# Eight convolution products in place of five rotary ones at the head of a mixer

## The chip, the cores and the metric

The kernel runs on one core of a Trainium2 chip. The metric is the device time of one execution in microseconds, as the median of the runs shown. All times below are microseconds (us) unless marked ns.

## The reference, cut to what matters

Two transformer blocks are computed on 512 tokens of width 1024, in float32. The change lies in the first block's mixer, which follows its first feed-forward part:

```
u = rms_norm(h, mix_pre_g)                  # one factor per token, a gain per channel
proj = u @ w_in                             # 1024 x 4808
q_a, k_a, v_a, q_i, k_i, w_i, gate_b, gate_c, conv_in, g_a, g_b = split(proj)
q_a, k_a, q_i, k_i = (apply_rope(t) for t in ...)
y_a = dsa_attention(q_a, k_a, v_a, q_i, k_i, w_i) @ w_a_out
y_b = (gate_b * short_conv_causal(gate_c * conv_in)) @ w_b_out
merged = sigmoid(g_a) * y_a + sigmoid(g_b) * y_b
h = h + rms_norm(merged @ w_out, mix_post_g)
```

`dsa_attention` scores every earlier token with the index heads (`q_i`, `k_i`, weighted by `w_i`), keeps the 128 best per query, and attends to these alone.

## The kernel before, in words

Activations lie with channels on the 128 partitions and the 512 tokens along the row. A product of 1024 input channels with 128 output channels is eight blocks of 128 channels. Every float32 factor is split into a high and a low part, and each block is three matmuls (`mm3`, line 287), so one product over all tokens is 24 matmuls of 512 columns (`lin`, line 296), and over one half of the tokens 24 matmuls of 256 columns. Each weight tile is loaded by a DMA on the sync queue, copied to the high part on ScalarE (line 252 or 282) and split on VectorE (line 253 or 283).

A stage begins in `begin` (line 303). The residual `h` is not complete then: the stage before it left behind a post-norm of its result `f` (`due`), and the second-half products of its last five output tiles (`self.rest`). `enter` (line 604) gives for each half of the tokens a list of steps: the sum of squares of `f`, its factor, the factor turned into a row, the update of `h` and the split of `h` into the next products' inputs (`body`, lines 624 to 633), and then the same three steps for the norm of `h`. The gain goes into the split, but the factor per token, `r`, does not: the products are begun on the unscaled `h`, and whoever takes a product out of PSUM multiplies by `r`. `begin` therefore runs a few products (their number is the length of `K["lead:mix"]`, whose letters say from which pool their weights are taken) over the first half, while the norm of the second half is prepared, and then over the second half. What takes a product out of PSUM (`put`) is held back until `r` of its half exists (lines 336 to 343). PSUM has five banks for these products ("lg" 3, "mm" 2, line 141).

In the mixer (line 939) the five lead products are the keys (T_KK, attention and index keys together) and four tiles of index queries (T_QI). Each is turned by `rotated` (line 774): four ScalarE copies with swapped halves (line 785), a VectorE product with the cosine table (787), a GpSimd product with the sine table (790), a VectorE sum (791). The factor `r` is multiplied into the two tables by GpSimd (`more`, line 946), once for each half. After the lead comes T_VW (values and index weights), over all tokens, and is scaled by `r` on VectorE (line 930). Then `keys` and `heads` split the turned tiles (lines 802 to 815), the index scores are made (lines 978 to 982; line 981 needs the index weights), and four tiles of attention queries (T_QA) follow. For each of three query blocks a chain of 16 rounds on VectorE finds the 128 best scores (lines 992, 993, ended by line 994). Under it TensorE does the convolution's twelve products (lines 1002 to 1015: gate_c, conv_in and gate_b for four tiles) and the first four gate products. `gate_c * conv_in` is taken without `r`, and the square of `r` (`rr`, line 1001) is multiplied in afterwards (line 1006); the two taps are line 1012.

Then eight attention units follow, two for each of four query blocks (line 1027): logits (lines 823, 824), softmax, transposes, products with the values. The first block needs no chosen scores, block 1 needs those of the first chain, and so on. With each unit one gate product is written (`gates`, line 1046: a product, a ScalarE copy, a GpSimd product with `r` at line 928, a tanh), and the second set of eight gates comes behind the units.

The order in the text isn't the order on the engines. When the kernel is built, the framework's scheduler takes for each engine the earliest written instruction that its own model of time holds to be ready and that finds a free tile. Tiles come from pools with fixed numbers of slots: 32 of "b", 8 of "t", 5 of "u" (line 60), 5 pairs of "w4" for weights. Gates, keys, queries, scores and outputs of the attention are all "b".

Of the kernel before, what the change touches and what calls it, by code (L numbers as in the profile page):

```python
# [15 lines left out]
OP = mybir.AluOpType  # L16
# [34 lines left out]
T_KK, T_QI, T_VW, T_QA, T_CONV, T_GB, T_GA = 0, 1, 5, 6, 10, 22, 30  # L51
# [35 lines left out]
 'urg:mixsh': 1,  # L87
 'sq:mixsh': 'PV',
 'bf:mix': [0, 1, 4, 6],
 'lead:mix': 'ubbbb',  # L90
 'ahead:mix': 5,
 'late:mix': [5, 0],
 'urg:crosssf': 1,
# [85 lines left out]
class Net:  # L179
# [123 lines left out]
    def begin(self, jobs, step, fill=()):  # L303


        first, second = step(A), step(B)
        wts = []
        for (w, n, xs, k0, _), tag in zip(jobs, K["lead:" + self.phase]):
            wts.append(self.lead_weights(w, n, len(xs), k0, tag) if tag != "w" else self.weights(w, n, len(xs), k0)[0])
        todo = first["post"] + first["body"] + first["norm"][:1]  # L310
        for go in self.rest:
            if todo:
                todo.pop(0)()
            go()
        self.rest = []
        for do in todo:
            do()
        todo = (second["post"][:2] + first["norm"][1:2] + second["post"][2:] + first["norm"][2:]
                + second["body"] + second["norm"])

        def advance():
            if todo:
                todo.pop(0)()

        for go in fill:
            go()
            advance()
        for _ in range(3):
            advance()

        for tok, d in zip(HALVES, (first, second)):
            waiting = []
            for (_, _, xs, _, put), wt in zip(jobs, wts):
                waiting.append((put, self.lin(wt, xs, tok)))
                advance()
                if not any(do in todo for do in d["norm"]):
                    while waiting:
                        put, ps = waiting.pop(0)
                        put(ps, tok)
            while any(do in todo for do in d["norm"]):  # L340
                advance()
            for put, ps in waiting:
                put(ps, tok)
        for do in todo:
            do()
# [573 lines left out]
    def projection(self, w, n, xs, r, alloc=None, light=False):  # L919

        nc = self.nc
        t = (alloc or self.tmp)((P, S), F32)

        def put(ps, tok):
            if light:
                nc.scalar.copy(t[:, tok], ps)  # L926
                if r is not None:
                    nc.gpsimd.tensor_tensor(t[:, tok], t[:, tok], r[:, tok], op=OP.mult)  # L928
            else:
                nc.vector.tensor_tensor(t[:, tok], ps, r[:, tok], op=OP.mult)  # L930

        return t, (w, n, xs, 0, put)

    def project(self, *args, **kw):
# [4 lines left out]
    def mix(self):  # L939
        self.phase = "mix"  # L940
        nc, h = self.nc, self.h
        cos, sin, cm = self.table("cos1"), self.table("sin1"), self.table("causal")

        def more(tok, r, rs):
            for t in (cos, sin):
                nc.gpsimd.tensor_tensor(t[:, tok], t[:, tok], r[:, tok], op=OP.mult)

        xs, r, step = self.enter("mix_pre_g", more)
        w = "w_in"
        turns = [self.rotated(w, n, xs, cos, sin) for n in (T_KK, T_QI, T_QI + 1, T_QI + 2, T_QI + 3)]  # L950
        vw, last = self.projection(w, T_VW, xs, r)
        self.begin([j for _, j in turns], step)
        self.stream([last])
        self.attending = True
        kk = turns[0][0]
        ka, ki = self.keys(kk, 0), self.keys(kk, 1)
        qi = []
        for x, _ in turns[1:]:
            qi += self.heads(x)
        v = []  # L960
        wi = self.small("wi", [P, NT, H], 1)
        for j in range(NT):
            ps = self.pa()
            nc.tensor.transpose(ps[:, :72], vw[:72, j * P : j * P + P], self.ident[:72, :72])
            v.append(self.values(ps[:, 0:64], j))
            nc.vector.tensor_scalar(wi[:, j, :], ps[:, 64:72], float(np.float32(H ** -0.5)), None, op0=OP.mult)


        first = self.cp.tile([P, P], F32, tag="first", name="first")
        nc.gpsimd.tensor_copy(first, cm[:, 384:512])  # L970
        bias = [first]
        score = []
        for i in range(1, NT):
            n = (i + 1) * P
            sc = self.big((P, n), F32)
            for hd in range(H):
                ps = self.bank("lg")
                self.logits(ps, qi[hd], hd % 2, i, ki, n)
                t = self.tmp((P, n))
                nc.scalar.activation(t, ps[:, :n], AF.Relu, scale=0.125)  # L980
                nc.vector.scalar_tensor_tensor(
                    sc, t, wi[:, i, hd : hd + 1], cm[:, 384 - i * P :] if hd == 0 else sc, op0=OP.mult, op1=OP.add)
            score.append(sc)
        qa = []
        for t in range(4):
            x, job = self.rotated(w, T_QA + t, xs, cos, sin)
            self.stream([job])
            qa += self.heads(x)
        for sc in score:
            for _ in range(TOPK // 8):  # L990
                m8 = self.small("m8", [P, 8], 4)
                nc.vector.max(out=m8, in_=sc)
                nc.vector.match_replace(out=sc, in_to_replace=m8, in_values=sc, imm_value=TAKEN)
            nc.vector.tensor_scalar(sc, sc, TAKEN_BELOW, NEG, op0=OP.is_gt, op1=OP.mult)
            bias.append(sc)


        self.second = nc.gpsimd if K["conv"] == "P" else nc.vector
        bz = []
        rr = self.rowtile()  # L1000
        nc.gpsimd.tensor_tensor(rr, r, r, op=OP.mult)
        for j in range(4):
            c = self.project(w, T_CONV + 3 * j, xs, None, light=True)
            ci = self.project(w, T_CONV + 3 * j + 1, xs, None, light=True)
            nc.gpsimd.tensor_tensor(c, c, ci, op=OP.mult)
            nc.gpsimd.tensor_tensor(c, c, rr, op=OP.mult)
            tap = [self.gains[:, G_CONV + 3 * j + d : G_CONV + 3 * j + d + 1] for d in range(3)]
            z = self.tmp()
            nc.scalar.activation(z, c, AF.Copy, scale=tap[2])
            for d in (1, 0):  # L1010
                s = 2 - d
                nc.vector.scalar_tensor_tensor(z[:, s:], c[:, : S - s], tap[d], z[:, s:], op0=OP.mult, op1=OP.add)
            b = self.project(w, T_CONV + 3 * j + 2, xs, r, light=True)
            nc.gpsimd.tensor_tensor(b, b, z, op=OP.mult)
            bz.append(self.split(b, self.pair()))

        self.second = nc.vector


        ot = [self.big(dt=F32) for _ in range(4)]  # L1020
        gb, more_b = self.gates(w, T_GB, xs, r, KD)
        ga, more_a = self.gates(w, T_GA, xs, r, KD)

        for _ in range(K["gb0"]):
            next(more_b)

        def units():
            for i in range(NT):
                for g in range(2):
                    yield self.group(i, g, qa, ka, v, ot, (i + 1) * P,  # L1030
                                     lambda l, hd, j: self.softmax(l, 0.125, (i + 1) * P, bias[i], pool=K["F6"][j])), [lambda: next(more_b, None)]

        self.overlapped(units())
        for _ in more_b:
            pass
        for _ in more_a:
            pass
        self.attending = False
        self.branch(gb, "w_b_out", bz)
        merged = self.merge(gb, ga, "w_a_out", [self.split(t, self.pair(alloc=self.xt)) for t in ot])  # L1040
        f = [self.big(dt=F32) for _ in range(KD)]
        self.memory_parts()
        self.down("w_out", f, 0, merged, False, K["late:mix"])
        self.leave(f, "mix_post_g")
# [589 lines left out]
```

## Time and profile before

| | |
|---|---|
| runs | 2095.65, 2098.32, 2098.66 us, median 2098.32 |
| profiled execution | 2091.38 us, of which the span from first to last instruction is 2089.6 |
| busy, share of the span | TensorE 96%, its weight loads 85%, VectorE 74%, ScalarE 53%, GpSimd 12% |
| mean granted TensorE clock | 0.990 of full speed |
| mixer, head: lead products and T_VW | 361 to 415 us |
| mixer, scores and choice of the best | 417 to 539 us |
| mixer, attention units and gates | 539 to 640 us |

A busy TensorE in this table is one whose matmuls overlap in the profile's records; their ends are modelled. The granted clock has two levels, full and half; a value in between is a mean over a stretch.

### The profile page before, as it was taken

The numbers are of one execution on the slowest core, as the hardware profiler recorded it, in microseconds if no ns is written. First come the engines' busy times: TensorE is split into PE (matmuls) and PEld (weight loads), VectorE is DVE, ScalarE is ACT, GpSimd is POOL, SyncE is SP. The second block draws the span as 40 slices with busy tenths as digits, with TensorE's granted clock in tenths as the row PEclk, the third lists the DMA queues.
The fourth block names the chain that finished last, engine by engine and source line by source line (L and its number), as shares of the span: only waits on it lengthen the run. The fifth ranks groups of instructions, "written<-read, shape, count | busy, mean of one in ns | idle before, by whom it ended". The sixth has DMA issues, their size and how long they took to land. (4 is left out here: it accounts for less than half of the span.)

```text
span 2089.6 us, 32337 instructions
## 1 busy us (share of the span) xinstructions
PE 2011.4 (96%) x12428; PEld 1766.1 (85%) x12428; DVE 1544.4 (74%) x2956; ACT 1101.7 (53%) x2052; POOL 254.4 (12%) x239
## 2 busy tenths in 40 slices
PE   8999999899999999999999998998999999999997
PEld 7899998778778888998999998776778888988997
DVE  7977786799775585587777869588987678666755
ACT  5644454673573454554445445467864436444752
POOL 2000002313331310040000003213100000000001
PEclk9999999899999999999999999999999999999999
DMA  5233333212222233221333342211112313323331
GB/s 163 91 112 97 106 107 122 71 61 91 91 71 95 77 120 103 93 70 51 113 110 102 106 141 72 66 41 51 41 41 81 114 31 122 99 89 104 112 101 41
DMA packets 66010, 186.43 MB, mean 89 GB/s; under 512 B 6976, under 2 KB 14144, under 8 KB 65856
## 3 DMA queue, kind: packets, MB, share of 16 engines
q1 hardware_dynamic: 63376, 180.97, 26.8%
q10 hardware_dynamic: 2448, 3.41, 0.5%
q8 instruction: 97, 1.59, 0.3%
q14 instruction: 57, 0.47, 0.1%
q0 software_dynamic: 32, 0.00, 0.0%
HBM read 182.25 MB, written 2.10 MB: 88 GB/s over the span
## 5 line engine op out<-in xcount | busy, mean ns | idle before, releaser
L290 PE MATMUL mm<-x,w 128*128 128x512 f32 (+1 forms) x2064 | 473.8, 379 | 0.0
L290 PE MATMUL mm<-b,w 128*128 128x256 f32 (+1 forms) x2625 | 448.6, 322 | 2.0 <-ACT b L510 1.8
L290 PEld LDWEIGHTS mm<-x,w 128*128 128x128 f32 x2064 | 364.0, 188 | 74.9 <-DVE v L1274 0.7
L290 PEld LDWEIGHTS mm<-b,w 128*128 128x128 f32 x2625 | 375.2, 188 | 48.9 <-ACT b L510 4.2
L252 ACT CAST w<-r 128x1024 fp32r<-128x1024 f32 (+2 forms) x256 | 229.8, 898 | 277.8 <-PE mm L290 118.0
L290 PE MATMUL lg<-x,w 128*128 128x256 f32 (+1 forms) x2460 | 348.6, 295 | 6.8 <-DVE t L1385 4.7
L253 DVE TENSOR_TENSOR w<-r,w 128x1024 fp32r<-128x1024 f32 (+2 forms) x254 | 267.8, 1055 | 116.3 <-ACT w L252 111.3
L290 PE MATMUL lg<-b,w 128*128 128x256 f32 (+1 forms) x1929 | 352.9, 334 | 0.0
L290 PEld LDWEIGHTS lg<-x,w 128*128 128x128 f32 x2460 | 315.9, 188 | 27.9 <-DVE t L1385 6.4
L290 PEld LDWEIGHTS lg<-b,w 128*128 128x128 f32 x1929 | 294.5, 188 | 42.1
L457 ACT CAST w<-r 128x1024 fp32r<-128x1024 f32 x147 | 154.6, 1053 | 138.1 <-PE lg L290 81.3
L458 DVE TENSOR_TENSOR w<-r,w 128x1024 fp32r<-128x1024 f32 x147 | 178.7, 1221 | 19.9 <-ACT w L457 19.4
L290 PE MATMUL mm<-x,u 128*128 128x256 f32 x756 | 108.1, 287 | 15.6 <-ACT x L513 7.1
L510 ACT CAST b<-t 128x512 fp32r<-128x512 f32 (+1 forms) x113 | 60.8, 539 | 112.5 <-DVE t L745 34.3
L290 PEld LDWEIGHTS mm<-x,u 128*128 128x128 f32 x756 | 96.9, 193 | 18.7 <-ACT x L513 7.5
L569 POOL TENSOR_TENSOR sh<-sh,sh 128x256 f32<-128x256 f32 x45 | 37.5, 834 | 502.8 <-ACT sh L563 499.9
L511 DVE TENSOR_TENSOR b<-t,b 128x512 fp32r<-128x512 f32 (+1 forms) x113 | 67.2, 596 | 26.3 <-ACT b L510 26.0
L569 POOL TENSOR_TENSOR sf<-sf,sf 128x256 f32<-128x256 f32 x28 | 23.3, 833 | 450.4 <-ACT sf L563 440.4
L563 ACT ACTIVATE sh<-h 128x256 f32<-128x256 f32 x128 | 49.9, 411 | 52.5 <-DVE h L630 22.7
L928 POOL TENSOR_TENSOR b<-b,rows 128x512 f32<-128x512 f32 x32 | 52.5, 1642 | 174.7 <-ACT b L926 174.7
L861 DVE TENSOR_TENSOR u<-tt,u 128x512 fp32r<-128x512 f32 x92 | 62.0, 684 | 9.9 <-ACT u L860 9.3
L290 PE MATMUL lg<-x,b 128*128 128x256 f32 x456 | 68.1, 291 | 0.0
(271 smaller groups left out, 2738.9 us busy)
## 6 DMA issues: line engine op xcount, KB each, us to landing
r<-in_ffn_w SPq DMA_DIRECT2D x86, 512.0 KB, 3.3
r<-in_w_in SPq DMA_DIRECT2D x64, 512.0 KB, 3.2
r<-in_ffn_w SPq DMA_DIRECT2D x68, 256.0 KB, 2.7
r<-in_w_up SPq DMA_DIRECT2D x32, 512.0 KB, 3.2
r<-in_w_down SPq DMA_DIRECT2D x32, 384.0 KB, 3.4
r<-in_ffn_w SPq DMA_DIRECT2D x16, 384.0 KB, 3.3
r<-in_w_out SPq DMA_DIRECT2D x8, 512.0 KB, 3.2
r<-in_xattn_w_k SPq DMA_DIRECT2D x8, 512.0 KB, 3.2
```

Of the source, the lines that this page charges most:

```text
L252: nc.scalar.copy(hi, raw)
L253: self.second.tensor_tensor(lo, raw, hi.bitcast(F32), op=OP.subtract)
L290: self.nc.tensor.matmul(ps, lhsT=lhsT, rhs=rhs, start=start, stop=stop, skip_group_check=on)
L457: nc.scalar.copy(hi, raw)
L458: nc.vector.tensor_tensor(lo, raw, hi.bitcast(F32), op=OP.subtract)
L510: nc.scalar.copy(hi, src)
L511: nc.vector.tensor_tensor(lo, src, hi.bitcast(F32), op=OP.subtract)
L563: nc.scalar.activation(t, x, AF.Square)
L569: eng.tensor_tensor(ts[0], ts[0], t, op=OP.add)
L861: nc.vector.tensor_tensor(lo, ps[:, :n], hi.bitcast(F32), op=OP.subtract)
L928: nc.gpsimd.tensor_tensor(t[:, tok], t[:, tok], r[:, tok], op=OP.mult)
```

## The change

Eight convolution products (gate_c and conv_in of four tiles) become the lead. They need no `r`, so `begin` takes them out of PSUM at once (the mark `free`), with a ScalarE copy into a "b" tile. The tables are loaded behind the lead and multiplied by `r` over all tokens; the products `gate_c * conv_in` are taken on GpSimd at the same place. The five rotary products then follow over all tokens, and T_VW after them as before. In the convolution's loop only gate_b is left to be multiplied out.

```
- 'lead:mix': 'ubbbb',
+ 'lead:mix': 'uttbbbww',
@@ begin
-                waiting.append((put, self.lin(wt, xs, tok)))
+                ps = self.lin(wt, xs, tok)
+                if getattr(put, "free", False):
+                    put(ps, tok)
+                else:
+                    waiting.append((put, ps))
                 advance()
@@ projection
+        put.free = light and r is None
         return t, (w, n, xs, 0, put)
@@ mix
+        xs, r, step = self.enter("mix_pre_g")
+        w = "w_in"
+        conv = [self.projection(w, T_CONV + 3 * j + d, xs, None, lambda shape, dt: self.big(shape, dt), True)
+                for j in range(4) for d in range(2)]
+        self.begin([j for _, j in conv], step)
+        conv = [t for t, _ in conv]
         cos, sin, cm = self.table("cos1"), self.table("sin1"), self.table("causal")
-        def more(tok, r, rs):
-            for t in (cos, sin):
-                nc.gpsimd.tensor_tensor(t[:, tok], t[:, tok], r[:, tok], op=OP.mult)
-        xs, r, step = self.enter("mix_pre_g", more)
-        w = "w_in"
+        for t in (cos, sin):
+            nc.gpsimd.tensor_tensor(t, t, r, op=OP.mult)
+        for j in range(4):
+            nc.gpsimd.tensor_tensor(conv[2 * j], conv[2 * j], conv[2 * j + 1], op=OP.mult)
         turns = [self.rotated(w, n, xs, cos, sin) for n in (T_KK, T_QI, T_QI + 1, T_QI + 2, T_QI + 3)]
         vw, last = self.projection(w, T_VW, xs, r)
-        self.begin([j for _, j in turns], step)
+        self.stream([j for _, j in turns])
         self.stream([last])
...
         for j in range(4):
-            c = self.project(w, T_CONV + 3 * j, xs, None, light=True)
-            ci = self.project(w, T_CONV + 3 * j + 1, xs, None, light=True)
-            nc.gpsimd.tensor_tensor(c, c, ci, op=OP.mult)
+            c = conv[2 * j]
             nc.gpsimd.tensor_tensor(c, c, rr, op=OP.mult)
```

## Rows read from the trace of the kernel before

**Rows 1.** The page, busy time of each engine over the whole span.
```profile
PE 2011.4 (96%) x12428; PEld 1766.1 (85%) x12428; DVE 1544.4 (74%) x2956; ACT 1101.7 (53%) x2052; POOL 254.4 (12%) x239
```

**Rows 2.** Windows, head: length, busy (instructions) PE, PEld, DVE, ACT, POOL, clock, DMA.
```profile
361.14:370.71 9.57, 7.36 (x38) 6.56 (x37) 9.57 (x21) 7.10 (x17) 0.73 (x1) 0.71 0.35 110
370.71:383.72 13.01, 13.01 (x105) 12.80 (x104) 7.36 (x28) 6.13 (x14) 3.06 (x4) 0.95 0.32 111
383.72:388.15 4.43, 0.00 (x0) 0.03 (x1) 3.13 (x6) 1.94 (x5) 3.67 (x5) 0.72 0.08 33
388.15:400.86 12.71, 11.47 (x66) 10.51 (x66) 11.77 (x27) 9.76 (x23) 4.05 (x5) 0.69 0.01 1
400.86:414.79 13.93, 13.91 (x91) 12.17 (x89) 9.38 (x23) 10.86 (x27) 7.02 (x9) 1.00 0.21 75
414.79:421.65 6.86, 3.17 (x16) 2.25 (x17) 6.54 (x10) 6.62 (x16) 0.18 (x1) 1.00 0.01 1
421.65:433.75 12.10, 12.10 (x61) 9.91 (x59) 11.88 (x30) 10.27 (x24) 0.00 (x0) 1.00 0.14 45
```

**Rows 3.** TensorE's timeline: start, length, instructions, idle before and releaser.
```profile
388.15 0.55 PE L290 MATMUL mm<-x,u 128*128 128x256 f32 x1 [4.43 <-DVE t L787]
...
417.47 0.39 PE L823 MATMUL lg<-b,b 128*128 128x256 f32 x1 [2.69 <-DVE b L803]
```

**Rows 4.** Waits from 361 to 425: who for whom, total, times, longest.
```profile
PE mm L290 <- DVE t L787: 4.4, 1, 4.4
...
DVE t L787 <- POOL b L946: 3.2, 2, 1.9
```

**Rows 5.** VectorE's timeline at the end of the head.
```profile
419.60 0.69 DVE L930 TENSOR_TENSOR t<-lg,rows 128x512 f32<-128x512 f32 x1
...
425.16 9.12 DVE L981 SCALAR_TENSOR_TENSOR b<-t,wi,b 128x256 f32<-128x256 f32 x18
```

**Rows 6.** Windows of the choice and of the units up to query block 3.
```profile
425.16:538.99 113.83, 113.83 (x491) 91.94 (x492) 110.46 (x218) 54.27 (x82) 33.99 (x23) 1.00 0.25 84
538.99:583.50 44.51, 41.45 (x210) 33.86 (x209) 30.32 (x126) 29.92 (x70) 14.27 (x11) 1.00 0.25 83
```

**Rows 7.** VectorE's groups from 425.16 to 538.99: busy, mean ns, idle before.
```profile
L253 DVE TENSOR_TENSOR w<-r,w 128x1024 fp32r<-128x1024 f32 x17 | 25.0, 1469 | 0.0
...
L1012 DVE SCALAR_TENSOR_TENSOR t<-t,gains,t 128x511 f32<-128x511 f32 (+1 forms) x8 | 6.5, 814 | 0.0
```

**Rows 8.** Windows of line 290's matmuls alone: length, busy (instructions), clock, DMA.
```profile
414.79:433.75 18.96, 6.91 (x23) 1.00 0.09 29
433.75:538.99 105.24, 105.24 (x451) 1.00 0.26 85
538.99:571.33 32.34, 25.64 (x104) 1.00 0.28 92
571.33:583.50 12.17, 4.14 (x15) 1.00 0.17 59
...
616.49:640.20 23.71, 23.71 (x102) 1.00 0.33 106
```

**Rows 9.** Line 994, which ends a choice: durations, first and last start.
```profile
L994 DVE TENSOR_SCALAR b<-b x3: 283/352/426, 475.3 to 538.6; 128x256 f32<-128x256 f32 x1, 128x384 f32<-128x384 f32 x1, 128x512 f32<-128x512 f32 x1
```

**Rows 10.** TensorE's timeline: first logits of query blocks 0 and 3.
```profile
540.63 0.28 PE L823 MATMUL lg<-b,b 128*128 128x256 f32 x1
...
583.51 0.40 PE L823 MATMUL lg<-b,b 128*128 128x512 f32 x1
```

**Rows 11.** GpSimd's timeline: the squared factor of line 1001.
```profile
406.18 1.04 POOL L1001 TENSOR_TENSOR rows<-rows 128x512 f32<-128x512 f32 x1
```

**Rows 12.** Groups of the whole span: busy, mean ns, idle before and releasers.
```profile
L290 PEld LDWEIGHTS lg<-x,w 128*128 128x128 f32 x2460 | 315.9, 188 | 27.9 <-DVE t L1385 6.4 <-DVE t L741 3.4 <-ACT sh L474 2.6
...
L474 ACT COPY sh<-lg 128x256 f32<-128x256 f32 x98 | 35.7, 365 | 9.2 <-PE lg L290 9.0
...
L1005 POOL TENSOR_TENSOR t<-t,t 128x512 f32<-128x512 f32 x4 | 5.4, 1348 | 25.7 <-ACT t L926 25.7
```

## The prediction

> **What bounds the kernel now.** I read the page first. TensorE is busy 96% of the span [rows 1], so a gain is idle TensorE time that goes away, or matmuls that get cheaper. The slices point to the mixer's head, and windows cut there show why [rows 2]. A full stretch gives the pace of the half-token matmuls: 105 in 13.01 us, 0.124 us each [rows 2]. Over all tokens it is 102 in 23.71 us, 0.2325 each, or 5.58 us for a product of 24 [rows 8]. Against this pace the head loses time in four places:
> - 361.14 to 370.71: 38 matmuls are worth 4.7 of 9.57 us. They wait for the first half's inputs, at a mean clock of 0.71.
> - 383.72 to 388.15: 4.43 us with no matmul at all. The releaser is line 787 [rows 3, 4], the cosine product that frees a PSUM bank, and it waited on its part for GpSimd's line 946, the tables times the norm's factor [rows 4].
> - 388.15 to 400.86: 66 matmuls are worth 8.2 of 12.71 us, 4.5 lost, at a mean clock of 0.69. That is half clock in part, right behind the idle gap. VectorE is busy 11.77 us of it.
> - 414.79 to 421.65: TensorE is busy 3.17 of 6.86 us, 3.7 lost. The longest idle piece ends with line 803, the split of the turned queries [rows 3].
>
> Behind the head TensorE is full up to 538.99, and so is VectorE: 110.46 of 113.83 us [rows 6]. Here two engines bound the kernel at once, and that decides what the gain is worth.
>
> **What goes.** The conv products don't need the factor. ScalarE empties a bank as soon as its product is done, at 0.365 us for a copy of this shape [rows 12]; 16 of them are 5.8 us, spread over 48 us of products on an engine that the rotary copies leave. So 4.43 us go. The 4.5 us behind it should go nearly whole: the first half now has eight products instead of five, so the second half's inputs are made under three more products, while the rotary work of VectorE and GpSimd, which stood in between, has moved behind the lead. The 3.7 us go because five products stand between the keys and the first score. The loss at 361 stays. Removed: **12.6 us**.
>
> **What is added.** Three more products run in halves: 48 x 0.124 = 5.95 against 5.58 us, 0.37 each, **1.1 us** in all. The weights of eight lead products instead of five cost ScalarE and VectorE nothing more in sum, since the same tiles were split later before. Their loads move forward on the sync queue, past those of the keys; DMA is at most 0.35 busy there [rows 2], so I price this at nothing, and at one late load, some 3 us, if a slot is missing. The table loads move behind the lead, on ScalarE's queue; their first reader is the keys' put 48 us later. On GpSimd the four products of 1.35 us [rows 12] come ahead of the keys' sine product. GpSimd is nearly free there, and a delay falls on the turned keys, not on TensorE, which has five products to go.
>
> **What moves later.** TensorE's ledger from 370.71: of the first half 192 - 38 = 154 matmuls, 192 of the second, and 36 short ones of the norms (276 records in the head's first five windows less 240 for ten half products, T_VW's 24 left out), all at 0.124, are 47.4 us. The lead ends at 418.1. Five rotary products and T_VW are 33.5 us more, to 451.6. The index weights come out of T_VW, which is last; line 930 and a transpose follow, so the first score sum (line 981) starts at about **453.5**, where it was 425.16 [rows 5]. This is the price of the change: the choice of the best scores starts 28 us later.
>
> VectorE's ledger from there to the first logits of query block 3, which need the last choice (583.51 before [rows 10]): before, 110.46 + 30.32 = 140.8 us busy [rows 6]. Eight weight splits of 1.469 us [rows 7] have left it: -11.8. TensorE has more gates to do meanwhile (below), 1.3 splits: +1.9. The taps, 6.5 us [rows 7], have their inputs from about 420 on, when VectorE has little to do. The scheduler does take such work early: the squared factor, written behind the choice, ran at 406.18 [rows 11]. A tap needs a "t" tile, and there are eight; I take three tiles' taps out of four as moved, -4.9, with none and all as bounds. That leaves 126.0 us, at the old share of 0.970 (110.46 of 113.83) 129.9 us. Block 3 starts at **583.4**, with bounds of 588.4 and 581.7.
>
> TensorE's work until then: the scores, at most 9.9 us (3.17 + 12.10 busy from 414.79 to 433.75 [rows 2] less 23 x 0.2325 [rows 8]), eight products (44.6), units 0 to 2 (41.45 - 119 x 0.2325 = 13.8 [rows 6, 8]) and gates. Of the 32 "b" slots keys, queries, convolution and outputs hold 22, so ten gates can be done (55.8). From 451.6 that ends at 575.7. TensorE waits some 8 us for VectorE, so VectorE's ledger decides.
>
> **The sum.** Before, at 583.5, 23 + 451 + 104 + 15 = 593 matmuls [rows 8] are 24.7 products, 16 for queries and convolution and 8.7 gates; the rest of the mixer's gates ended at 640.20, 56.7 us later, with TensorE nearly full. With ten gates done the rest is 56.7 - 1.3 x 5.58 = 49.4 us, so it ends at 632.8, **7.4 us earlier**. In TensorE's terms: 12.6 less 1.1 is 11.5, and some 4 of them are given back to VectorE. The bounds of the taps give 2.4 and 9.1. Nothing behind the mixer changes. Against the profiled execution's 2091.4 us that is 2084; that execution lies 6.9 below the median of 2098.3, so for the median I say **2091**.
>
> **Rivals.**
> 1. *TensorE never waits.* Scheduler and VectorE keep up: 11.5 us stay, and the 3.1 us that TensorE idles from 538.99 to 583.50 [rows 6] go too: 14.6, **2084**. For it: the units there were late because products came first. Against: VectorE's sum. Chance 0.17.
> 2. *Slower: the units don't run under the choice.* Their logits stand behind the last line 994 before (540.63 against 538.6 [rows 9, 10]). If they stay there, the choice ends at 453.5 + (110.46 - 11.8 + 3.25 x 1.469) / 0.97 = 560.0, with seven gates done, all that the slots allow while the scores live. Units 0 to 2 then take between 33 us (13.8 + 16.7 for three gates, and the old 3.1 idle) and the old 44.5. Block 3 starts at 593 to 604.5, the gates end at 642 to 654, 2 to 14 us late: **2106**. It decides as soon as logits of block 0 start behind the last line 994. For it: order is fixed by a model, not by the run. Against: that TensorE had unbroken older work up to 540 explains the place before as well. Chance 0.19.
> 3. *Nothing gained.* The second half's update of `h` shares VectorE with the splits of two lead products more and comes late, so the 4.5 us return, and the score chain starts that much later still: 7.4 less 4.5 to 6, **2097**. For it: VectorE was busy 11.77 of 12.71 us there [rows 2]. Chance 0.12.
> 4. *Each weight load stands in the open.* Three more products in halves are 72 more loads of 0.188 us [rows 12], 13.5 us, **2104**. Against: 105 loads and matmuls in 13.01 us, 0.124 for a pair, less than a load alone, so they overlap. Chance 0.02. The Trainium skill, "TensorE: Matmul & The Clock Gate", section "The mechanism", says that a weight load overlaps running matmuls only when it targets other rows of the array, which full-height loads never do; by its columns / 1.2 ns the estimate is 72 x 107 ns, 7.7 us. The trace disagrees, by the pair of 0.124.
>
> **How the numbers follow.** My forecast has 0.50. A measurement of this kernel can tell some 0.2%, 4.2 us. Of the forecast 0.38 lie beyond that and 0.12 within, as its band reaches from 2089 to 2096. Faster: 0.38 + 0.17 = 0.55. Same: 0.12 + 0.12 + 0.01 of rival 2 = 0.25. Slower: 0.18 + 0.02 = 0.20. The range goes from 2082, just past rival 1, to 2106, the middle of rival 2, and leaves out its upper half and a rest, under 0.2.
>
> **What would show it.** In the changed profile: no idle piece above 1 us between 371 and 450, and no half clock there; the first line 981 at 450 to 456; lines 1012 for three tiles ahead of it; logits of block 0 ahead of the last line 994; block 3's first logits at 581 to 589; the last gate near 633. The forecast is wrong if line 981 comes much later than 456, if TensorE shows a gap of over 8 us between 540 and 590 with VectorE named, or if gates still run behind 640.

## The result, and the profile after

The changed kernel takes **2116.1 us** (median of 6, 2110.06 to 2119.66) against 2096.5 for the kernel before beside it (median of 6): a ratio of 1.0092, 95% interval 1.0080 to 1.0104. It is 19.6 us **slower**, where the prediction said 2091 with 2082 to 2106 as its range. The profiled execution has a span of 2114.6 us, 25.0 more than the one before; as single executions scatter, the medians are what is to be explained.

The page of the kernel after says little by itself, as TensorE is busy the same 96% [rows 1]:

```profile
PE 2025.4 (96%) x12500; PEld 1777.3 (84%) x12500; DVE 1540.3 (73%) x2947; ACT 1100.9 (52%) x2041; POOL 250.7 (12%) x232
```

A busy TensorE at half clock is busy twice as long, so I read four fixed windows around the mixer as length less busy time times granted clock: what TensorE lost there against full clock without a gap. The clock column is the mean of the whole window, idle time included, so a gap at half clock is partly counted twice; worked out piece by piece from the same traces, the losses differ by up to 3 us. First the kernel before, then the one after (columns as in [rows 2]):

```profile
360.00:440.00 80.00, 68.41 (x407) 60.45 (x406) 66.39 (x152) 57.30 (x128) 20.82 (x25) 0.89 0.16 53
440.00:500.00 60.00, 60.00 (x258) 48.32 (x258) 58.00 (x125) 29.96 (x43) 18.71 (x13) 1.00 0.29 96
500.00:600.00 100.00, 96.94 (x460) 78.39 (x459) 84.24 (x245) 55.26 (x115) 33.24 (x24) 1.00 0.22 75
600.00:680.00 80.00, 79.90 (x355) 64.13 (x355) 45.67 (x73) 36.20 (x60) 17.76 (x12) 1.00 0.31 99
```

```profile
360.00:440.00 80.00, 74.69 (x518) 70.48 (x517) 43.61 (x93) 35.69 (x75) 29.39 (x28) 0.94 0.21 70
440.00:500.00 60.00, 54.84 (x238) 44.45 (x237) 48.28 (x89) 43.50 (x77) 7.87 (x7) 0.94 0.20 63
500.00:600.00 100.00, 84.34 (x370) 65.60 (x368) 93.47 (x273) 45.55 (x95) 31.20 (x23) 0.93 0.14 47
600.00:680.00 80.00, 77.92 (x351) 60.90 (x351) 50.84 (x108) 45.28 (x82) 22.57 (x15) 1.00 0.34 112
```

Before, the four lose 19.1 (80 - 68.41 x 0.89), 0.0, 3.1 and 0.1 us; after, 9.8, 8.5, 21.6 and 2.1. **The head does get 9.3 us back. The next stretch gives 8.5 away, and the one from 500 to 600, where the query blocks run, 18.5.** With the last one, 2.0, the sum is 19.7, close to the 19.6 between the medians. That it fits so well is partly luck: the two executions profiled are 25.0 apart, and piece by piece the four windows differ by 18.7.

The three losing places, one by one. In the head, TensorE's timeline has a new gap right behind the first half of the lead, in front of the column sums of the second half's norm, and half clock behind it (windows, columns as in [rows 2]):

```profile
395.02 1.83 PE L586 MATMUL tt<-ones,sh 128*128 128x1 f32 x8 [3.67 <-DVE sh L575]
```

```profile
375.41:391.36 15.95, 15.95 (x136) 15.74 (x134) 14.59 (x39) 8.15 (x21) 5.87 (x7) 1.00 0.31 102
391.36:395.02 3.66, 0.00 (x0) 0.03 (x1) 3.41 (x10) 2.81 (x8) 0.00 (x0) 0.91 0.00 0
395.02:400.13 5.11, 5.11 (x24) 5.11 (x25) 1.71 (x10) 0.37 (x1) 0.00 (x0) 0.50 0.00 0
400.13:423.28 23.15, 23.15 (x193) 23.15 (x191) 1.23 (x1) 3.93 (x9) 11.58 (x10) 0.98 0.12 35
423.28:456.90 33.62, 33.62 (x147) 27.09 (x146) 18.43 (x23) 22.11 (x33) 8.52 (x6) 1.00 0.29 94
456.90:476.84 19.94, 14.78 (x66) 12.29 (x65) 15.40 (x33) 15.31 (x35) 1.27 (x1) 0.83 0.17 54
```

The lead ends at 423.28. While its last part runs (from 400.13), VectorE does 1.23 us of work in 23.15: it could have made scores or choices, and has none to make. At 456.90 the matmuls of the six products that follow the lead are through, and TensorE waits again: 5.16 us idle up to 476.84, part of the rest at half clock, 7.7 lost. ScalarE's timeline shows for what (per rotary product: four copies of line 789, the heads' copies of line 806, a weight copy of line 252):

```profile
450.14 2.40 ACT L789 ACTIVATE t<-mm 32x512 f32<-32x512 f32 x4
454.65 1.26 ACT L806 CAST b<-t 64x512 fp32r<-64x512 f32 x2 [2.12 <-DVE t L795]
455.94 1.05 ACT L252 CAST w<-r 128x1024 fp32r<-128x1024 f32 x1
457.02 2.39 ACT L789 ACTIVATE t<-lg 32x512 f32<-32x512 f32 x4
461.51 1.26 ACT L806 CAST b<-t 64x512 fp32r<-64x512 f32 x2 [2.11 <-DVE t L795]
```

ScalarE makes its copies, waits 2.1 us until GpSimd's sine product and VectorE's sum are back, and then copies the heads: from one line 789 to the next 6.88 us (457.02 - 450.14), where TensorE needs 5.58 for the product. From T_VW's last matmul to the first score sum pass 9.1 us (456.90 to 466.0). In the kernel before it was no less, 10.4 us (414.79 to 425.16); T_VW in TensorE's timeline, before and after:

```profile
409.02 5.77 PE L290 MATMUL lg<-x,w 128*128 128x512 f32 x24
```

```profile
451.28 5.76 PE L290 MATMUL mm<-x,w 128*128 128x512 f32 x24
```

The first score sum and the end of the choice, beside [rows 5, 9]:

```profile
L991 DVE SCALAR_TENSOR_TENSOR b<-t,wi,b x24: 472/609/1269, 466.0 to 483.7; 128x256 f32<-128x256 f32 x8, 128x384 f32<-128x384 f32 x8, 128x512 f32<-128x512 f32 x8
L1004 DVE TENSOR_SCALAR b<-b x3: 350/420/1053, 525.0 to 582.5; 128x256 f32<-128x256 f32 x1, 128x384 f32<-128x384 f32 x1, 128x512 f32<-128x512 f32 x1
```

The scores start at 466.0 instead of 425.16, the last choice ends at 582.5 instead of 538.6. Then TensorE's timeline, and VectorE's at the same moment:

```profile
542.95 0.28 PE L827 MATMUL lg<-b,b 128*128 128x256 f32 x1
...
553.66 0.58 PE L827 MATMUL lg<-b,b 128*128 128x256 f32 x1 [8.21 <-DVE sm_m L837]
...
599.49 0.48 PE L827 MATMUL lg<-b,b 128*128 128x512 f32 x1
```

```profile
551.86 0.68 DVE L1003 MATCH_REPLACE8 b<-m,b 128x512 f32<-128x512 f32 x1
552.45 0.35 DVE L1004 TENSOR_SCALAR b<-b 128x384 f32<-128x384 f32 x1
552.72 0.69 DVE L1002 MAX8 m<-b 128x8 f32<-128x512 f32 x1
553.32 0.27 DVE L837 CUSTOM_DVE_ANT_0 t<-lg,first 128x128 f32<-128x128 f32 x1
```

The last group of rows: VectorE's and TensorE's work between the first score sum and block 3's first logits, line 290's matmuls alone, and the first ones behind the mixer's gates:

```profile
466.00:599.49 133.49, 117.83 (x515) 93.14 (x514) 123.80 (x334) 70.03 (x138) 35.08 (x26) 0.94 0.14 48
```

```profile
456.90:599.49 142.59, 97.26 (x387) 73.24 (x386) 0.93 0.15 49
599.49:663.78 64.29, 48.78 (x191) 35.26 (x192) 1.00 0.35 115
```

```profile
663.78 2.96 PE L290 MATMUL lg<-b,w 128*128 128x512 f32 x12
```

Block 0 needs no choice at all, and its first logits run at 542.95, 40 us ahead of the last choice's end. But its softmax (line 837, which empties the logits' bank) stands in VectorE's queue behind the choice for block 2, which ends at 552.45. Until then the next logits have no bank, and the gates behind them in TensorE's queue wait too: 8.2 us. Matmuls that might have filled nearly half of them were there: a gate's product had begun at 543.65 with 7 of its 24 matmuls, and the other 17 stand right behind the logits.

A second gap of the same stretch has another reason. Three windows, and ScalarE's weight copies around them:

```profile
545.44:553.66 8.22, 0.01 (x2) 0.01 (x1) 8.08 (x20) 2.44 (x4) 1.26 (x1) 0.65 0.20 64
553.66:560.03 6.37, 6.37 (x20) 5.13 (x20) 6.37 (x26) 1.48 (x6) 0.00 (x0) 0.64 0.00 0
582.68:599.49 16.81, 11.20 (x53) 8.07 (x52) 13.77 (x64) 10.99 (x31) 4.33 (x4) 0.90 0.00 0
```

```profile
544.46 1.03 ACT L252 CAST w<-r 128x1024 fp32r<-128x1024 f32 x1
602.83 1.03 ACT L252 CAST w<-r 128x1024 fp32r<-128x1024 f32 x1
```

The first gap costs 10.5 us with the half clock behind it. From 582.68 to 599.49 another 6.7 are lost, and no gate can fill them: between these two lines ScalarE copies no weight tile, and TensorE has no gate matmul from 582.8 to 604.24. The DMA's share is 0.00 from 553.66 to 602.83, so the tile copied then had landed long before; its copy stands behind the softmax in ScalarE's queue. Whether the scheduler's order or a lack of free tiles put it there wasn't tested.

### The profile page after: what moved, and what is told of

It is laid out like the page before. It is cut to its first block, busy times and chain, and to the rows that moved or that the text cites. A ratio compares the mean times of both kernels' runs of the same rounds, so it can differ in the third digit from the quotient of the medians.

```text
span 2114.6 us, 32441 instructions
## 1 busy us (share of the span) xinstructions
PE 2025.4 (96%) x12500; PEld 1777.3 (84%) x12500; DVE 1540.3 (73%) x2947; ACT 1100.9 (52%) x2041; POOL 250.7 (12%) x232
## 5 line engine op out<-in xcount | busy, mean ns | idle before, releaser
L290 PE MATMUL mm<-x,w 128*128 128x512 f32 (+1 forms) x2064 | 466.9, 376 | 1.4 <-ACT b L930 1.4
L290 PE MATMUL mm<-b,w 128*128 128x256 f32 (+1 forms) x2553 | 435.2, 323 | 1.2 <-ACT b L514 0.9
L290 PEld LDWEIGHTS mm<-x,w 128*128 128x128 f32 x2064 | 359.2, 190 | 73.2 <-ACT b L930 1.9
L290 PEld LDWEIGHTS mm<-b,w 128*128 128x128 f32 x2553 | 367.5, 188 | 45.2 <-ACT b L514 1.9
L290 PE MATMUL lg<-b,w 128*128 128x256 f32 (+1 forms) x2001 | 368.5, 334 | 0.9 <-ACT b L514 0.9
L290 PE MATMUL lg<-x,w 128*128 128x256 f32 (+1 forms) x2484 | 356.9, 296 | 5.2 <-DVE t L1393 2.3
L290 PEld LDWEIGHTS lg<-x,w 128*128 128x128 f32 x2484 | 322.1, 188 | 27.7 <-DVE t L1393 4.0
L290 PEld LDWEIGHTS lg<-b,w 128*128 128x128 f32 x2001 | 303.7, 188 | 45.6 <-ACT b L514 2.3
L462 DVE TENSOR_TENSOR w<-r,w 128x1024 fp32r<-128x1024 f32 x147 | 178.6, 1220 | 21.8 <-ACT w L461 21.6
L290 PE MATMUL mm<-x,u 128*128 128x256 f32 x732 | 102.9, 289 | 9.4 <-ACT x L517 7.2
L567 ACT ACTIVATE sh<-h 128x256 f32<-128x256 f32 x128 | 50.0, 411 | 51.9 <-DVE h L634 22.4
L290 PE MATMUL lg<-x,b 128*128 128x256 f32 x456 | 62.8, 285 | 0.0
```

What stands on the lines that cost most here:

```text
L290: self.nc.tensor.matmul(ps, lhsT=lhsT, rhs=rhs, start=start, stop=stop, skip_group_check=on)
L462: nc.vector.tensor_tensor(lo, raw, hi.bitcast(F32), op=OP.subtract)
L567: nc.scalar.activation(t, x, AF.Square)
```

## The experiments

Three theories, as the expectations name them. **Late choice**: the loss comes from the scores' start at 466.0; VectorE's choice ends late, and TensorE runs out of work. **Head**: the products ahead of the rotary ones cost time in the lead and in the products behind it, and the choice has room to be late. **Queue**: block 0's logits stand in TensorE's queue ahead of gates that could run.

Every kernel ran beside the kernel before on the same chip, 4 to 12 times; the ratio goes by that neighbour, whose medians were 2095.9 to 2097.2. "Lost" is worked out as above, from the windows 360 to 440, 440 to 500, 500 to 600 and 600 to 680 of each run's profile; "first sum" is the first score sum, "choice" the start of the last instruction of the choice, in us of the profiled execution, one for each kernel. Every edit also lets the scheduler order the rest anew.

| kernel | median us | ratio (95%) | first sum | choice | lost |
|---|---|---|---|---|---|
| before | 2096.5 | | 425.2 | 538.6 | 19.1, 0.0, 3.1, 0.1 |
| changed | 2116.1 | 1.0080-1.0104 | 466.0 | 582.5 | 9.8, 8.5, 21.6, 2.1 |
| e1 changed, half the choice | 2100.3 | 1.0005-1.0028 | 467.5 | 545.5 | 10.0, 8.5, 8.2, 0.4 |
| e2 before, half the choice | 2093.2 | 0.9967-0.9994 | 426.2 | 498.3 | 18.5, 0.0, 1.1, 0.1 |
| e3 changed, T_VW first | 2118.9 | 1.0087-1.0121 | 466.4 | 585.2 | 8.9, 6.4, 21.9, 2.2 |
| e4 changed, 8 gates ahead | 2112.5 | 1.0061-1.0094 | 464.2 | 579.4 | 9.8, 8.5, 18.6, 6.1 |
| e5 changed, 4 lead | 2109.2 | 1.0036-1.0074 | 448.5 | 561.8 | 14.8, 8.4, 15.2, 0.1 |
| e6 before, 2 ahead | 2107.8 | 1.0028-1.0062 | 436.5 | 550.6 | 22.4, 0.0, 10.1, 0.1 |
| e7 before, 4 ahead | 2104.6 | 1.0013-1.0040 | 445.5 | 556.5 | 12.6, 2.6, 12.4, 0.1 |
| e8 changed, sine on VectorE | 2111.0 | 1.0039-1.0071 | 462.5 | 575.7 | 9.4, 0.8, 20.0, 1.2 |
| e9 before, scores later | 2110.1 | 1.0051-1.0092 | 454.8 | 555.1 | 20.9, 5.5, 9.2, 0.1 |
| e10 = e8, half the choice | 2092.8 | 0.9971-0.9998 | 461.7 | 536.7 | 9.8, 0.8, 5.2, 0.8 |
| e11 before, sine on VectorE | 2097.7 | 1.0003-1.0023 | 424.8 | 539.9 | 18.7, 1.3, 2.7, 0.1 |
| e12 = e7, sine on VectorE | 2105.6 | 1.0031-1.0070 | 442.1 | 562.4 | 12.9, 1.8, 17.1, 0.1 |
| e13 before, 1 behind | 2100.0 | 1.0007-1.0027 | 427.4 | 542.0 | 17.6, 0.8, 2.7, 0.1 |
| e14 before, 2 behind | 2101.8 | 1.0012-1.0036 | 434.5 | 546.2 | 19.3, 0.6, 6.8, 0.1 |

**e1 and e2: half the choice, in both kernels.**

```diff
-            for _ in range(TOPK // 8):
+            for _ in range(TOPK // 16):
```

> The changed kernel with 8 rounds in place of 16 in each choice of the best scores; the other 8 rounds are left out. Late choice (the loss is that the first score sum starts at 466.0 instead of 425.2, so that VectorE's choice ends late and TensorE runs out of work beneath it): some 28 us of VectorE work leave the critical stretch, the time falls to 2090 to 2098, within 4 us of the kernel before cut in the same way. Head (the loss is made in the lead and the rotary products themselves, by 423 to 477): the choice is beside the point, the time stays 15 us or more above the kernel before cut in the same way.

> The kernel before with 8 rounds in place of 16; the other 8 are left out. Late choice: TensorE was full beneath the choice there, so little is gained: 2086 to 2094, and the gap to the changed kernel cut likewise closes from 20 us to under 4. Head: the same 2086 to 2094 here, but the gap stays at 15 or more.

The kernel before gains 3.7 us (2096.8, the median of its 19 runs beside these, less 2093.2), the changed one 15.8 (2116.1 - 2100.3). So the gap shrinks from 19.6 to 7.1 us, which neither theory had expected (under 4, or 15 and more), and the loss from 500 to 600 from 21.6 to 8.2: some 13 us of the loss are the choice that ends late. The 8.5 of the stretch ahead of it stay.

**e3: the index weights' product T_VW ahead of the rotary ones.**

```diff
+        self.stream([last])
         self.stream([j for _, j in turns])
-        self.stream([last])
```

> The changed kernel with T_VW ahead of the five rotary products, nothing else. The index weights are then ready some 28 us earlier, and the score sums can begin with the first query tile, near 445 instead of 466. Late choice: 2098 to 2108. Head: the same products in another order, 2112 to 2119.

The time is in Head's range, and the first score sum didn't move (466.4). But the index weights didn't come earlier either: T_VW's product did, yet its transposes (line 974) ran at 455.81, behind the last rotary product, and line 976 wrote the weights at 465.92. So the run doesn't tell whether the scores wait for the weights; it tells that the place of T_VW's matmuls isn't what makes them late. ScalarE's queue was left: the values' copy, and line 990 that hands the scores on, stand behind the last rotary product's copies.

**e4: eight gates ahead of the query blocks instead of four.**

```diff
- 'gb0': 4,
+ 'gb0': 8,
```

> The changed kernel with eight gate products written ahead of the attention units in place of four. Queue (TensorE's idle 8.2 us at 545 come because the logits of block 0 stand ahead of gates that could run): these 8 us go, 2104 to 2110. Late choice: TensorE has the gates done earlier but block 3 still waits for the last choice, so at most 4 us change: 2112 to 2120.

At the lower end of Late choice's range. The wait behind block 0's logits goes to a later place (574.48) and becomes longer (the waits of TensorE from 500 to 640, in the changed kernel and in e4: total, times, longest):

```profile
PE lg L827 <- DVE sm_m L837: 9.0, 4, 8.2
```

```profile
PE lg L827 <- DVE sm_m L837: 11.6, 3, 9.9
```

By the medians the earlier gates are worth 3.6 us, but the two intervals overlap, so even that isn't sure. As the wait stayed, the run doesn't show what TensorE would gain without it; where it lies, the gap costs 10.5 us in the changed kernel.

**e5 to e7: fewer convolution products in the lead.** e5 is the changed kernel with the products of two tiles in the lead and the other two back in the loop behind the choice. e6 and e7 are the kernel before, with two and four such products put ahead of the five rotary ones in one lead (e6's core):

```diff
- 'lead:mix': 'ubbbb',
+ 'lead:mix': 'ubbbbww',
...
-        self.begin([j for _, j in turns], step)
+        conv = [self.projection(w, T_CONV + 3 * j + d, xs, None, lambda shape, dt: self.big(shape, dt), True)
+                for j in range(1) for d in range(2)]
+        self.begin([j for _, j in conv] + [j for _, j in turns], step)
```

> The changed kernel with four convolution products in the lead in place of eight; the other two tiles' four products go back to their place behind the choice. Late choice: four products of 5.6 us each leave the stretch ahead of the scores, so the first score sum comes some 22 us earlier than 466.0, at 441 to 447, the choice ends some 22 us earlier than 582.5, and the time is 2098 to 2106. Head (what was lost was lost in the first products and the rotary loop, and both stay): the first score sum moves as far, but the time stays at 2112 to 2118.

> The kernel before with two convolution products, taken without the factor, put ahead of its five rotary ones in the lead; the rotary tables are still scaled by halves, and all eight follow in one lead. Late choice: two products are 11 us of TensorE, and some 6 to 8 us of the lead's 12.6 us of idle are filled by them, so the first score sum comes 3 to 6 us later than 425.2 and the choice is barely late; what the filled idle gives back comes through at the end: 2088 to 2094. Head (the products without the factor cost the lead itself, by a late start and half clock): the idle is only moved, the first score sum comes 9 to 12 us later, 2096 to 2103.

> The same with four convolution products ahead of the five rotary ones. Late choice: 22 us of products against at most 12.6 us of idle, so the first score sum comes 10 to 14 us later than 425.2, which the stretch beneath the choice partly takes: 2091 to 2098. Head: 18 to 22 us later, 2100 to 2106.

e5's scores start 17.5 us earlier than the changed kernel's, its stretch from 500 to 600 loses 6.4 less, but its head 5.0 more: 2109.2, between the two theories. e6's scores start 11.3 us later, as Head had it, and its time is beyond both theories: two products cost 11 us. e7 is in Head's range with both numbers (20.3 us later, 2104.6), but not for Head's reason: its head loses 6.5 less than the kernel before, and the stretch from 500 to 600 loses 9.3 more. So Head is right that the lead hardly hides the products, and Late choice that in e5 and e7 the price is paid behind. Of the three only e6's head itself loses more than before, 22.4 against 19.1. Its timeline, TensorE's lines around the gap:

```profile
388.00 2.99 PE L290 MATMUL lg<-x,w 128*128 128x256 f32 x24
396.65 0.56 PE L586 MATMUL tt<-ones,sh 128*128 128x1 f32 x2 [5.66 <-DVE sh L575]
398.57 0.77 PE L290 MATMUL lg<-x,b 128*128 128x256 f32 x2 [1.36 <-DVE t L791]
```

With more products in the lead the small matmuls of the second norm still wait on VectorE's squares; the idle moved there and grew. It was no free room: TensorE waits there for VectorE's work on the second half (line 575's sums of squares), and more products in front don't shorten that work.

**e8 and e11: the sine products of the five rotary products on VectorE**, in the changed kernel and in the one before.

```diff
-            nc.gpsimd.tensor_tensor(y[:, tok], y[:, tok], sin[:, tok], op=OP.mult)
+            (sine or nc.gpsimd).tensor_tensor(y[:, tok], y[:, tok], sin[:, tok], op=OP.mult)
...
+        turns = [self.rotated(w, n, xs, cos, sin, sine=nc.vector) for n in (T_KK, T_QI, T_QI + 1, T_QI + 2, T_QI + 3)]
```

> The changed kernel with the sine products of the five rotary products moved from GpSimd to VectorE, which is nearly idle there. Loop (per rotary product ScalarE makes four copies, waits 2.1 us until GpSimd's product and VectorE's sum are back, then makes the heads' copies, 6.9 us a product against TensorE's 5.6): the wait falls by about 1 us a product, the first score sum comes 4 to 6 us earlier, at 460 to 462, and the time falls by 2 to 5 us to 2111 to 2114. Elsewhere (the loop is no limit; the scores wait for the values product's place in ScalarE's queue): the first score sum stays at 465 to 467 and the time at 2115 to 2118.

> The kernel before with the sine products of its five first rotary products on VectorE, which is some 80 per cent busy there. If a wait for GpSimd's product paces its lead too, the first score sum comes 1 to 3 us earlier and the time is 2093 to 2096; if VectorE is what its lead waits for, the sums come later and the time is 2097 to 2102.

ScalarE's timeline in e8, where its wait was 2.1 us:

```profile
446.97 1.26 ACT L806 CAST b<-t 64x512 fp32r<-64x512 f32 x2 [1.07 <-DVE t L795]
448.26 2.39 ACT L789 ACTIVATE t<-mm 32x512 f32<-32x512 f32 x4
...
452.70 2.40 ACT L789 ACTIVATE t<-lg 32x512 f32<-32x512 f32 x4
455.13 1.27 ACT L806 CAST b<-t 64x512 fp32r<-64x512 f32 x2
```

The wait halves or goes, the loss from 440 to 500 falls from 8.5 to 0.8, and the time by 5.1 us: the round trip is shown. The scores come only 3.5 us earlier, just short of the 4 to 6 expected, so the late choice stays nearly whole (20.0). In e11 the same edit gains nothing (1.0013): GpSimd's product doesn't pace that lead. The scores start where they did (424.8), not later, as the second case had it, so that VectorE is what the lead waits for there is argued, from its 66.39 busy of the 80 us to 440, and not shown.

**e9: the kernel before, with the scores later and nothing else.** The four T_QA products stand ahead of the scores instead of behind them.

```diff
+        qa = []
+        for t in range(4):
+            x, job = self.rotated(w, T_QA + t, xs, cos, sin)
+            self.stream([job])
+            qa += self.heads(x)
         bias = [first]
         score = []
...
-        qa = []
-        for t in range(4):
-            x, job = self.rotated(w, T_QA + t, xs, cos, sin)
-            self.stream([job])
-            qa += self.heads(x)
         for sc in score:
```

> The kernel before with its lead untouched, and the four T_QA rotary products put ahead of the scores in place of behind them: nothing is added or removed, only the scores and the choice start some 22 to 26 us later. Late choice (in the runs so far TensorE's idle and half clock between 500 and 600 us is 3 us where the choice ends at 538.6, 10 at 550.6, 12 at 556.5, 15 at 561.8, 20 at 582.5, about half a microsecond for each): the choice ends at 560 to 566, the stretch loses 13 to 17 us, and the time is 2106 to 2112. Head (the loss lies in the lead): the lead is as before, so 2095 to 2099.

The time is 2110.1, 14.2 us more, by order alone and with the old lead. That shows that later scores cost time by themselves, and rules out Head as the whole cause. Of the 14.2 us, 6.1 lie in the stretch from 500 to 600, 5.5 in the one before and 1.8 in the head's window. The scores started 29.6 us later instead of 22 to 26, yet the choice ended earlier than expected (555.1; T_QA's rotary work, which used to run between its rounds, was already done), so the stretch from 500 to 600 lost 9.2 instead of 13 to 17; and four rotary products over all tokens without scores among them lost 5.5 in the stretch before, as the changed kernel's five do.

**e10: the changed kernel with both repaired** (e8's edit and half the choice).

> The changed kernel with the sine products of its five first rotary products on VectorE and with 8 rounds of the choice in place of 16 (it leaves half of the choice out). If the late choice and ScalarE's loop are the whole loss, both are out: TensorE loses 7 to 10 us in the lead against 18 before, 0 to 2 from 440 to 500, 3 to 7 from 500 to 600, and the time is 2090 to 2095, level with the 2093.2 of the kernel before with half the choice. If something else in the change costs (the extra products in halves, the start of the lead), it stays at the 2100.3 of the changed kernel with half the choice, 2098 to 2102.

```profile
360.00:440.00 80.00, 74.66 (x516) 70.49 (x515) 43.98 (x94) 35.61 (x74) 26.40 (x25) 0.94 0.21 70
440.00:500.00 60.00, 59.21 (x267) 47.63 (x266) 56.01 (x105) 47.57 (x83) 6.85 (x5) 1.00 0.22 71
500.00:600.00 100.00, 94.84 (x450) 75.87 (x449) 87.24 (x260) 59.56 (x126) 38.49 (x25) 1.00 0.23 74
```

2092.8, level with the 2093.2 of e2. All four numbers of the first theory came, and the gap is closed: ScalarE's loop and the late choice are what turns the change into a loss. Even then next to nothing is won. The head loses 8.7 less than e2's (9.8 against 18.5); 4.1 of that go from 500 to 600 (5.2 against 1.1), 0.8 and 0.7 in the other two stretches, and 1.1, by the prediction's term, to the three products in halves. Some 2 us would be left; the medians differ by 0.4. Against its own neighbour each gained 3.1 (e10) and 3.7 (e2), so no gain is shown.

**e12 to e14: can a version win?** e12 is e7 with e8's edit. e13 and e14 put one and two convolution products behind the rotary ones in the lead, so that the scores needn't wait for them (e14's core; e13 takes only the first of the two):

```diff
-        self.begin([j for _, j in turns], step)
+        self.begin([j for _, j in turns] + [j for _, j in conv], step)
```

> Four convolution products without the factor ahead of the five rotary ones in one lead, with the sine products on VectorE. Late choice: the first score sum at 438 to 445 in place of 445.5, the choice ends 2 to 7 us earlier than 556.5, the time is 2099 to 2103. Head: VectorE is the lead's limit, the sums come no earlier, 2103 to 2108.

> The kernel before with one convolution product, taken without the factor, put behind the five rotary ones in each half of the lead, where TensorE stood idle for 4.4 us at 383.7 and for several microseconds up to 421.7; its eleven other products stay where they were. Order (the change lost because its products stood ahead of the rotary ones, and so of the scores; idle behind them can be filled for nothing): the head loses 3 to 6 us less, the first score sum stays at 425 to 428, and the time is 2091 to 2095. Presence (TensorE's idle in the lead is VectorE's work, which a product more doesn't shorten, and a product in the lead only puts the next wait behind it): the head's idle falls, but the scores start 4 to 6 us later, and the time is 2097 to 2101.

> The same with two convolution products behind the five rotary ones. Order: the head loses 6 to 10 us less, the scores start at 426 to 431, 2089 to 2095. Presence: the scores start 9 to 12 us later, 2102 to 2108, as with two products ahead of the rotary ones (2107.8).

None beats the kernel before. e12's scores came 3.4 us earlier than e7's, as Late choice said, but its choice ended 5.9 later, and the time is in Head's range. Between first sum and choice VectorE was busy 114.1 us instead of 106.9, most of it for two more weight splits (line 253: 16 in 25.8 us instead of 14 in 19.2), and idle 6.2 instead of 4.1; why the splits came there stays open. e13 is undecided: its scores are nearly in place (427.4) and its four windows lose 21.2 against 22.3, on Order's side, though its head gives back 1.5 instead of 3 to 6; its time is 3.0 us more, in Presence's range. In the four windows that doesn't show, and its cause stays open. e14 is 4.8 us slower and its scores start 9.3 later, on Presence's side.

**All runs together** show how the loss goes with the choice's end. In the order of the choice's end, the loss from 500 to 600 is 1.1 (498), 3.1 (539), 2.7 (540), 2.7 (542), 6.8 (546), 10.1 (551), 9.2 (555), 12.4 (557), 15.2 (562), 17.1 (562), 20.0 (576), 21.6 (583), 21.9 (585). The changed kernels with half the choice lie above it at 537 and 546 (5.2 and 8.2), e4, whose gates moved, below it (18.6 at 579). Up to 542 a later choice goes with nearly no loss; from there to 562 with some 0.6 us for each microsecond ((15.2 - 2.7) / (561.8 - 542.0) = 0.63), as an estimate from one execution of each kernel. The kernel before sits just ahead of that bend.

## Why the prediction was wrong

- **What bounds the kernel: right.** Two engines bound it behind the head, and the late choice decides the worth of the gain. The sign was lost in the size of the delay and in the gates left over.
- **What goes, 12.6 us: too much.** The window to 440 lost 9.3 less, and part of that only moved. The gap at 383.72 went, but "the second half's inputs are made under three more products" failed: VectorE, 14.59 busy of 15.95 us there, finished the second half's squares too late, and 3.67 us of idle and half clock for 5.11 us (2.6 lost) took the place of the old piece. That is close to the condition of rival 3, which I gave 0.12. The 3.7 us in front of the scores didn't go either: they came back behind T_VW as 7.7 (456.90 to 476.84). The mixer's first matmul also came at 364.04 instead of 361.14; the feed-forward layer's tail waits there, and why wasn't tested.
- **The price, 28 us: the step that failed.** It was 40.8 (466.0 - 425.2), 12.5 more than the sum has. 5.2 of them are the lead's end (423.3 for 418.1): the gap and half clock above are 6.2, the late start 2.9, and what took some of that back wasn't separated. "Five rotary products and T_VW are 33.5 us more" was right for TensorE (33.62 from 423.28 to 456.90). The other 7.2 are the way from T_VW's last matmul to the first score sum. The sum gives it 1.9 us (451.6 to 453.5), with "line 930 and a transpose follow", and it took 9.1; the kernel before had taken 10.4, from the end of the window at 414.79 [rows 2] to 425.16 [rows 5]. What I left out is the rotary products' own round trip: ScalarE needs 6.9 us for each, and the last line 789 began when TensorE was through. e8, which shortens that trip, brings the 9.1 to 5.4 (457.1 to 462.5), so about half of the 7.2 is shown to be it; the rest stays open.
- **VectorE's ledger: the sum right by luck, the share wrong.** From the first score sum to block 3's first logits VectorE was busy 123.8 us; the forecast was 126.0. Two errors cancel in it: all taps stayed (8.1 us instead of 1.6), and of the 23 weight splits before, 10 were left on VectorE, not 16.3, 16.0 us where the sum has 22.4 (line 253, 425.16 to 583.50 before and 466.00 to 599.49 after):

```profile
L253 DVE TENSOR_TENSOR w<-r,w 128x1024 fp32r<-128x1024 f32 x23 | 32.3, 1403 | 5.2 <-ACT w L252 4.6 <-PE tt L858 0.6
L253 DVE TENSOR_TENSOR w<-r,w 128x1024 fp32r<-128x1024 f32 x10 | 16.0, 1602 | 0.0
```

And it took 133.5 us instead of 129.9, a share of 0.93 instead of 0.97. Block 3 started at 599.5 instead of 583.4: 12.5 from the start, 3.6 from the longer stretch.
- **The taps: wrong.** The squared-factor products did run early on GpSimd (408 to 427), but the taps (now line 1020) began between 503.1 and 522.7, under the choice, though VectorE had 1.23 us of work from 400.13 to 423.28.
- **Ten gates done by then: wrong.** Line 290 has 387 matmuls from 456.90 to 599.49, less eight products 8.1 gates. So 8.0 were left where I had six, and the gates ended at 663.8, 64.3 us after block 3 began instead of 49.4. "TensorE waits some 8 us for VectorE" was some 25: 7.7 around the first scores, 10.5 at block 0's logits with a gate ready behind them, 6.7 from 582.68 on with no weights copied for one. So this step failed as well, and it weighs as much as the price: the mixer's last gate came 31.0 us later than the 632.8 forecast, 12.5 from the scores' start, 3.6 from VectorE's stretch and 14.9 from the gates left over. It is also why rival 1, TensorE never waiting, fell.
- **Rival 2** had the sign, 0.19 and almost block 3's start (593 to 604.5). Its condition did not come true: block 0's logits ran under the choice. The tie to the choice was the softmax, in VectorE's queue; "logits of block 0 ahead of the last line 994" was on my list as a good sign, and is none.
- **Rival 4** stays out: the half-token products of the lead run 193 matmuls in 23.15 us, 0.120 each, against 0.188 for a load.
- **The list of signs** did its work: line 981 (now 991) past 456, a gap over 8 us between 540 and 590 with VectorE named, gates behind 640. All three came.

## What to carry to other kernels

Price a product that is moved by the slowest engine of its round trip, here ScalarE's copies and its wait for the way back, and not by its matmuls alone. Price the way from the last matmul to the first reader too, from the rows of the kernel before: here it had been 10.4 us. Before filling an idle TensorE, look at who ends that idle: if the work behind it feeds an engine that is already full further on, a microsecond won in front can be worth less than a microsecond of its delay. A unit that starts early on one engine helps only as far as its next step isn't behind the long work in another engine's queue.

## What was not expected of the hardware

After 3.67 us without a matmul TensorE's granted clock was 0.50 for the next 5.11 us, though it had been 1.00 and full for the 15.95 before: 1.2 instead of 2.4 GHz, and a gap of 3.7 us cost 6.2. I had expected the half clock behind 388.15 [rows 2] to go with its gap; the new gap brought its own.
